# All c, x, query and gate columns of a decoder layer as pairs by seven products, with the attention beside the gates' pairs

## The chip, the cores and the metric

The kernel runs on one core of one Trainium2 chip. The metric is the device time of one execution in microseconds (us): the time before is the median of 3 runs, 964.23 us (963.68 to 964.24). The trace is of one more execution, which took 963.59 us.

The engines are named as the profile names them: PE is TensorE's matmuls and PEld its weight loads, DVE is VectorE, ACT is ScalarE, POOL is GpSimd, and SP is SyncE, which here only issues DMAs. Each engine takes its instructions in one order and waits at the first that isn't ready.

## The reference

One layer of a decoder, for a prompt of 512 tokens and 8 sequences of 8 new tokens, which are computed together as 576 columns. What matters of it here:

```
h = _rmsnorm(x, norm1_g) * (1.0 + sc1) + sh1
proj = h @ w_in
b_gate, c_gate, xa, q, k, v, ga, gb = jnp.split(proj, cuts, axis=-1)
u = c_gate * xa
uc, new_conv = _causal_conv(u, conv_buf, conv_w)
ya = (b_gate * uc) @ w_conv_out
o, k_state, v_state = attend(q, k, v, attn_sinks)
yb = o @ w_attn_out
mixed = jax.nn.sigmoid(ga) * ya + jax.nn.sigmoid(gb) * yb
x = x + g1 * (mixed @ w_mix_out)
h2 = _rmsnorm(x, norm2_g) * (1.0 + sc2) + sh2
a, val = jnp.split(h2 @ w_up, 2, axis=-1)
x = x + g2 * ((gelu(conv(a)) * val) @ w_down)
```

The model's width is 1024, so `b_gate`, `c_gate`, `xa`, `q`, `ga` and `gb` are 1024 columns each, in 8 blocks of 128; `k` and `v` are 256 columns each. Attention has 16 heads of 64 with a window of 128. The outputs are both `y`, the last two inputs of both convolutions, and the last 128 rows of keys and values. All of it is float32.

## The kernel before, in words

**Products.** Tensors lie with their 1024 columns on the partitions (8 blocks of 128, "k") and the 576 tokens along the row. Every large product is made of three passes over numbers split in a high and a low part (fp32r): high weight by high input, high by low, low by high. A weight block (raw, 128x1024, 512 KB from DRAM on SP's queue, a ring of 4) becomes `whi` by an ACT copy and `wlo` by a DVE subtraction. Where a name is in `moved`, `wlo` is instead an ACT copy of the negated `whi`, to which a DMA from POOL's queue adds the raw block in place. `whi` and `wlo` are rings of 5.

**A plain product** (`product`) gives 128 output columns: 8 k by 3 passes by 2 groups of tokens (256 and 320) = 48 matmuls.

**A pair by seven products** (`pair_product`) gives two blocks of 128 output columns (a and b), by Winograd's form of the 2x2 block product: the tokens in two halves of 288, k in two halves of 4, and seven parts of 4 k by 3 passes = 12 matmuls of 288 tokens, 84 in all, where two plain products take 96. It needs sums of the inputs, made once for the layer (`x00`, `n1`, `t2`, `x10`, `n3`, `x11`, `n4`), and sums of the two weight blocks, made for each pair on DVE (six instructions of 128x512). The weights are split as A (parts a0 and a1), B (s1 and b1), C (s2 and s4) and D (s3, half as wide). The parts run in this order, on three banks X, Y and Z, and behind each part one instruction empties or starts a bank (bank, weights, inputs, what follows):

```
(X, "a0", "x00", lambda: minus(Y, X)),
(Z, "s1", "n1", lambda: act.activation(p5, Z, AF.Copy, scale=scale)),
(Y, "s2", "t2", lambda: minus(Z, Y)),
(X, "a1", "x10", lambda: out_a0(X)),
(Y, "s3", "n3", lambda: out_b1(Y, p5, ALU.subtract)),
(Z, "s4", "x11", lambda: out_a1(Z, p5, ALU.add)),
(Y, "b1", "n4", lambda: out_b0(Y)),
```

`minus` is an ACT copy of 128x288 from one bank to the next with the sign turned; part 3 adds onto Y = -X, so it waits for the first of them, which has part 2 (s1) to run beside; part 6 adds onto Z = -Y in the same way, with parts 4 and 5 between. Both are called the minus copies below. While a pair runs, `Job.prepare` gives the splits of the next pair to its steps: A and the first sums ahead of part 1, B behind part 1, D and the second sums behind part 3, C behind parts 4 and 5. X and Y lie in the pool `mm` and in `aux`; with `apart` both are in `mm`. The transposes and scores of the attention use `aux`.

**Order of the work.** After the norm come v, k, and two plain products of queries (128 columns each, q0 and q1). Then a loop over six m (`PLAIN` = 0, 1, 2, 4, 5, 6) makes c and x of block m as two plain products, multiplies them, and starts that block's convolution. In its turns 1 to 3 stand three pairs of queries. The attention is a generator (`fill`) from which `tick` takes pieces between matmuls at a rate (.32 in the plain products, .2 in the query pairs). Then come 14 pairs (`jobs`): the b columns with the convolution's output (`branch`), the sigmoid gates (`gate_job`), and c and x of blocks 3 and 7 as two pairs (`inner_job`); then four pairs of `w_conv_out`, eight plain products of `w_attn_out`, the mix, and the feed-forward part with its own 22 convolutions. PE is held to the program's order throughout (the wrapper `InOrder`, whose line 113 stands for all engines' instructions that go through it); ACT and DVE are pinned so from the last turn of the `PLAIN` loop on, and before that a scheduler orders them.

**Gates.** A gate pair empties its banks through ACT's sigmoid into `sg` and stores it to DRAM (`sg_dram`, 288 KB from POOL's queue). `gate` loads it back as `gt`: in `conv_outs` for the convolution branch (`late` multiplies, one job later), and two products ahead in the loop over `w_attn_out`.

Of the kernel before, what the change touches and what calls it, by code (L numbers as in the profile page):

```python
# [10 lines left out]
F32 = mybir.dt.float32  # L11
# [20 lines left out]
PLAIN = (0, 1, 2, 4, 5, 6)  # L32
Q_TICKS = 8
OPS_AT = 1, 2, 3, 4
CACHE_AT = 17,18
EPS = 1e-6
NEG = -1e33
A_BUFS = 57
# [35 lines left out]
def step_kernel(ctx: ExitStack, tc: tile.TileContext, ins: dict, outs: list):  # L74
# [19 lines left out]
    def slot(s, dt=F32, shape=None):  # L94
        return ap_.tile(shape or [P, NT], dt, tag="a", name=nm(s))

# [201 lines left out]
    class EarlyOperands(PairOperands):  # L298


        def high(self):
# [5 lines left out]
            if self.kp % 2 == 0:  # L307
                for n in ("n4", "n3"):
                    made[n] = slot(n + "h", F32R), slot(n + "l", F32R)
# [4 lines left out]
            self.n3h, self.n3l = (x[:, at] for x in made["n3"])  # L314
            act.activation(self.nh, self.r[0][:, a], AF.Copy)
            act.activation(self.n3h, self.r[0][:, b], AF.Copy)
# [10 lines left out]

        def low(self):
            for lo, src, hi in (
                (self.tl, self.t, self.th), (self.nl, self.r[0][:, :HT], self.nh),  # L330
                (self.n3l, self.r[0][:, HT:], self.n3h),
            ):
                dve.tensor_tensor(out=lo, in0=src, in1=hi.bitcast(F32), op=ALU.subtract)
# [555 lines left out]
    made = {}  # L889
    for i in range(5):  # L890
        if i in OPS_AT:
            EarlyOperands(h, OPS_AT.index(i), made, xn).all_early()
# [63 lines left out]
    ps = product(weights(kpm(w_in, Q0 + P), NK), h)  # L956
    q1 = slot("q")
    nc.scalar.activation(q1, ps, AF.Copy, scale=HD**-0.5)
    queries(1, q1)
# [88 lines left out]
    def decode_scores(q, s, cV):  # L1048
        kTc = []
        for raw, v in (caches[q][:2], caches[q][2:]):  # L1050
# [9 lines left out]
            yield False  # L1060
        s += [slot("s", shape=[P, 2, 256]) for _ in range(2)]
# [125 lines left out]
    def attention():  # L1187
        units = [(hd, i) for hd in range(4) for i in range(4)]
        s, pts = {}, {}
        for n in range(len(units) + 3):  # L1190
            if n in CACHE_AT:
                cache_load(CACHE_AT.index(n))
# [11 lines left out]
        filler[1] = .35  # L1204
# [11 lines left out]
    def padded():  # L1216
        t = slot("pad", shape=[P, 594])
# [6 lines left out]
    def conv(u, w0, w1, w2, st):  # L1224

        nc.gpsimd.tensor_copy(out=b10(u)[:, :, 0:2], in_=st)
        y = slot("y", shape=[P, 594])
# [87 lines left out]
    def beside_conv():  # L1315
        yield from attention()
        filler[1] = 40 / 84
# [3 lines left out]
    fill(beside_conv(), .3)  # L1321
# [4 lines left out]
    class Job:  # L1326


        def __init__(self, mat, c, ops, outs, apart=P):
            self.mat, self.c, self.ops, self.outs, self.apart = mat, c, ops, outs, apart  # L1330
            self.before, self.after = {}, {}
# [18 lines left out]
    def branch_outs(*ms):  # L1350
        ts, ys = [slot("g") for _ in range(2)], [ycv.pop(m) for m in ms]

        def first_half(e, ps):
            dve.tensor_tensor(out=ts[e][:, :HT], in0=ps, in1=ys[e][:, :HT], op=ALU.mult)

        def second_half(e, x, y, op):
            t, v = ts[e], ys[e]
# [9 lines left out]

    def gate_outs(x, m):
        ta, tb = (slot("sg") for _ in range(2))

        def sigmoid(out, src):
            act.activation(out, src, AF.Sigmoid)

        def b1(x, y, op):
            dve.tensor_tensor(out=tb[:, HT:], in0=x, in1=y, op=op)

        def a1(x, y, op):
            sigmoid(tb[:, HT:], tb[:, HT:])
            dve.tensor_tensor(out=ta[:, HT:], in0=x, in1=y, op=op)

        def b0(ps):
            sigmoid(tb[:, :HT], ps)
            sigmoid(ta[:, HT:], ta[:, HT:])
            for e, t in enumerate((ta, tb)):
                pool.dma_start(sg_dram[x, m + e], t)

        return lambda ps: sigmoid(ta[:, :HT], ps), a1, b0, b1
# [15 lines left out]

    def gate(x, m):
# [6 lines left out]
    def conv_outs(m):  # L1411
# [4 lines left out]
            lambda t=t, g=g: dve.tensor_tensor(out=t, in0=t, in1=g, op=ALU.mult) for t, g in zip(ts, gs)  # L1416
# [37 lines left out]
    def gate_job(n):  # L1454
        x, c, m = (1, 5632, 2 * n) if n < 4 else (0, 4608, 2 * n - 8)
        return Job(w_in, c + m * P, made, lambda: gate_outs(x, m))

    jobs = [
        branch(0, 1), branch(2, 4), branch(5, 6), gate_job(0), gate_job(1), gate_job(2), inner_job(3),
        inner_job(7), gate_job(3), branch(3, 7), gate_job(4), gate_job(5), gate_job(6), gate_job(7),  # L1460
    ]
    n_conv = len(jobs)
    jobs += [Job(wco, m * P, made_g, lambda m=m: conv_outs(m)) for m in range(0, NK, 2)]


    for at, m in enumerate(PLAIN):
        if at in (4, 5):
            src, dst = ((ins["cache_k_win"], nks), (ins["cache_v_win"], nvs))[at - 4]
            tc.keep_in_program_order(
                nc.gpsimd.dma_start(  # L1470
                    dst[:, 0:120, :].rearrange("b (x w) c -> b x (w c)", x=2),
                    src[0].rearrange("b w h d -> b w (h d)")[:, 8:128, :].rearrange(
                        "b (x w) c -> b x (w c)", x=2
                    ),
                )
            )
        w = weights(kpm(w_in, 1024 + m * P), NK)
        if 1 <= at <= 3:
            qt = [slot("q") for _ in range(2)]
            filler[1] = .2  # L1480
            pair_product(q_job.w, made["op"], {}, *copy_outs(qt, HD**-0.5), True, HD**-0.5)
            filler[1] = .32
            for n in range(2):
                queries(2 * at + n, qt[n])
        if at == 5 and filler:
            filler[1] = .4
# [792 lines left out]
```

## Time and profile before

| | |
|---|---|
| time before, median of 3 runs | 964.23 us (963.68 to 964.24) |
| the profiled execution | 963.59 us |
| its span, first to last instruction | 961.5 us |
| PE / PEld busy in the span | 945.7 / 904.6 us |
| DVE / ACT / POOL busy | 713.8 / 538.4 / 120.3 us |
| granted TensorE clock | 0.997 |

The program's stretches in that execution: from 72.8 us on the plain products of c and x, with the query pairs and the attention between; from some 228 us the 14 pairs; from some 410 us the `w_conv_out` pairs, `w_attn_out` and the mix; from some 545 us the feed-forward part.

How to read the rows: names are those of the kernel without their numbers, out<-in; all seven-product and attention work goes through line 113 except what has a line of its own. A matmul's duration (295 ns for 288 tokens) is its way through the array and overlaps the next; what one costs is the distance from start to start. "Idle before" is the time an engine stood still ahead of an instruction, with the engine that ended it behind the arrow.

### The profile page before, as it was taken

The page shows a single profiled execution, that of the slowest core. Times are in us where ns is not written, and L with a number is a line of the kernel's source. Part 1 is how long each engine was busy: PE and PEld are TensorE (multiplying, and loading weights), DVE is VectorE, ACT ScalarE, POOL GpSimd, SP SyncE. Part 2 cuts the span into 40 slices and gives each one's busy share as a digit, 9 for nine tenths or more (in the row PEclk, how much of TensorE's full clock was granted, in tenths as well). Part 3 has the DMA queues.
Part 4 walks back from the last instruction along what each step waited for, and adds up shares of the span by engine and source line. Part 5 has one row for each costly group of instructions (what it writes and reads, how often), then busy time and mean ns, then how long its engine had stood idle before and what let it go on. Part 6 is the DMA issues. An engine that isn't in the chain of part 4 may idle for free.

```text
span 961.5 us, 18628 instructions
## 1 busy us (share of the span) xinstructions
PE 945.7 (98%) x7290; PEld 904.6 (94%) x7290; DVE 713.8 (74%) x1335; ACT 538.4 (56%) x1039; POOL 120.3 (13%) x297
## 2 busy tenths in 40 slices
PE   6999999999999999999999999999999999999997
PEld 5799898989899989999889999999999999999997
DVE  4786878764866767776677688995559998968874
ACT  5464647645666446875335567563226565546664
POOL 2121000101211011210001131100000001101110
PEclk9999999999999999999999999999999999999999
DMA  9992212425555768899985732332323333328542
GB/s 279 326 263 74 64 51 67 152 84 134 133 136 164 250 217 216 201 241 275 312 292 118 179 93 66 89 108 69 106 86 95 89 88 102 92 75 176 130 96 99
DMA packets 181689, 141.45 MB, mean 147 GB/s; under 512 B 7368, under 2 KB 161804, under 8 KB 181314
## 3 DMA queue, kind: packets, MB, share of 16 engines
q1 hardware_dynamic: 172546, 111.72, 38.9%
q0 software_dynamic: 8912, 28.29, 12.8%
q8 instruction: 57, 0.93, 0.4%
q14 instruction: 30, 0.25, 0.1%
q10 hardware_dynamic: 144, 0.26, 0.1%
HBM read 113.89 MB, written 12.07 MB: 131 GB/s over the span
## 4 chain that ended last, share of the span: by engine, by line
PE 71%; ACT 2%; DMA 1%; DVE 1%; issue 0%; DVEq 0%; ACTq 0%
PE mm L113 40%; PE aux L113 29%; PE aux L1270 2%; DMA wl<-s 1%; ACT whi L113 0%; ACT wlo L113 0%; ACT xh L113 0%; ACT s L1017 0%; ACT sg L113 0%; ACT nh L113 0%; DVE g L113 0%; DVE wlo L113 0%; ACT aux L113 0%; ACT p L113 0%; DVE s L1081 0%
## 5 line engine op out<-in xcount | busy, mean ns | idle before, releaser
L113 ACT ACTIVATE whi<-raw 128x1024 fp32r<-128x1024 f32 (+3 forms) x186 | 188.5, 1022 | 82.1 <-DVE raw L113 29.0
L113 DVE TENSOR_TENSOR wlo<-raw,whi 128x1024 fp32r<-128x1024 f32 (+2 forms) x163 | 192.4, 1186 | 40.9 <-ACT whi L113 40.3
L113 PE MATMUL aux<-2h,whi 128*128 128x288 f32 (+2 forms) x232 | 68.5, 295 | 0.0
L113 PE MATMUL aux<-2h,wlo 128*128 128x288 f32 (+2 forms) x232 | 68.4, 295 | 0.0
L113 PE MATMUL aux<-2l,whi 128*128 128x288 f32 (+2 forms) x232 | 68.3, 295 | 0.0
L113 DVE TENSOR_TENSOR raw<-raw 128x512 f32<-128x512 f32 x88 | 61.6, 700 | 2.8
L113 PE MATMUL mm<-hh,whi 128*128 128x256 f32 (+2 forms) x264 | 62.1, 309 | 0.5 <-ACT hh L113 0.5
L113 PE MATMUL mm<-hh,wlo 128*128 128x256 f32 (+2 forms) x264 | 58.2, 295 | 0.0
L113 PE MATMUL aux<-hh,whi 128*128 128x288 f32 (+1 forms) x196 | 57.7, 301 | 0.0
L113 PE MATMUL mm<-hl,whi 128*128 128x256 f32 (+2 forms) x264 | 57.4, 296 | 0.1
L113 PE MATMUL aux<-hl,whi 128*128 128x288 f32 (+1 forms) x196 | 56.5, 295 | 0.0
L113 PE MATMUL aux<-hh,wlo 128*128 128x288 f32 (+1 forms) x196 | 56.5, 295 | 0.0
L113 PEld LDWEIGHTS mm<-hh,whi 128*128 128x128 f32 x264 | 43.6, 188 | 6.6 <-issue 5.4
L113 PE MATMUL mm<-fh,whi 128*128 128x256 f32 x224 | 47.9, 295 | 0.1
L113 PE MATMUL mm<-fl,whi 128*128 128x256 f32 x224 | 47.9, 295 | 0.0
L113 PE MATMUL mm<-fh,wlo 128*128 128x256 f32 x224 | 47.7, 294 | 0.0
L113 PEld LDWEIGHTS mm<-hl,whi 128*128 128x128 f32 x264 | 44.0, 188 | 0.7 <-DVE hl L113 0.5
L113 PEld LDWEIGHTS mm<-hh,wlo 128*128 128x128 f32 x264 | 44.6, 188 | 0.0
L113 PEld LDWEIGHTS aux<-2l,whi 128*128 128x128 f32 x232 | 43.7, 188 | 0.0
L113 PEld LDWEIGHTS aux<-2h,whi 128*128 128x128 f32 x232 | 43.6, 188 | 0.0
L113 PEld LDWEIGHTS aux<-2h,wlo 128*128 128x128 f32 x232 | 43.6, 188 | 0.0
L113 DVE SCALAR_TENSOR_TENSOR y<-pad,par2T,y 128x592 f32<-128x592 f32 x44 | 36.7, 833 | 8.7 <-ACT y L113 7.9
(402 smaller groups left out, 3063.8 us busy)
## 6 DMA issues: line engine op xcount, KB each, us to landing
raw<-in_w_in SPq DMA_DIRECT2D x52, 512.0 KB, 4.6
raw<-in_w_up SPq DMA_DIRECT2D x44, 512.0 KB, 4.0
ada<-in_w_ada SPq DMA_DIRECT2D x64, 256.0 KB, 5.7
wlo<-raw POOLq DMA_DIRECT2D x17, 512.0 KB, 4.8
ad<-in_w_ada SPq DMA_DIRECT2D x32, 256.0 KB, 6.6
raw<-in_w_down SPq DMA_DIRECT2D x16, 512.0 KB, 4.0
sg_dram<-sg POOLq DMA_DIRECT2D x16, 288.0 KB, 4.4
gt<-sg_dram SPq DMA_DIRECT2D x16, 288.0 KB, 6.0
```

Source lines behind the costliest of these rows:

```text
L113: done = getattr(self.engine, name)(*args, **kwargs)
L1270: done = nc.tensor.matmul(ps[32 * j : 32 * j + 32, :], cT[:, k, :], cols[k][j], start=(k == 1), stop=(k == NK - 2),)
```

## The change

- c and x of all eight blocks are made by pairs (`inner_job` for m = 0 to 7: c and x of one block are the pair's two outputs). The six turns with plain products are gone, and `PLAIN` with them.
- One list of 23 pairs follows q1: gates 0, query pair 1, gates 1 and 2, query pair 2, gates 3 and 4, query pair 3, then `inner_job` and `branch` pairs, and gates 5 to 7 at the end. The four `w_conv_out` pairs follow as before.
- The attention is taken from beside these pairs (rates .28, .45 for the new tokens' part, .6 for the modulation behind it). For the first 14 (`N_ATT`) X and Y are both in `mm`, the low part of B is `moved`, and ACT and DVE are ordered by the scheduler; from the 15th on both are pinned, and the low parts of B and D are `moved`.
- Gate pairs copy raw sums to `sg` and DRAM. The sigmoid is one ACT instruction of 128x576 on each `gt` that comes back, in `late` and in the loop over `w_attn_out`.
- The split input n3 (behind x00's operands) no longer has tiles of its own: its high and low part overwrite the second halves of h's, after q1's product.
- Pads and convolution outputs (594 wide) have a pool of 5 tiles of their own; the pool of 576-wide slots goes from 57 to 54. The loads of the caches, the copies of the caches to the outputs and `state_out` move to other places.

```diff
-PLAIN = (0, 1, 2, 4, 5, 6)
+N_ATT = 14
-A_BUFS = 57
+A_BUFS = 54
+U_BUFS = 5
+    def wide(s):
+        return ap_.tile([P, 594], F32, tag="uy", name=nm(s), bufs=U_BUFS)
...
-                ("x00", h0, l0, a), ("n3", *made["n3"], at), ("x10", h1, l1, a), ("x11", h1, l1, b),
+                ("x00", h0, l0, a), ("n3", h0, l0, b), ("x10", h1, l1, a), ("x11", h1, l1, b),
...
-    fill(beside_conv(), .3)
+    fill(beside_conv(), .28)
...
+    def gate_outs(x, m):
+        ts = [slot("sg") for _ in range(2)]
+        a0, a1, b0, b1 = copy_outs(ts)
+
+        def last(ps):
+            b0(ps)
+            for e, t in enumerate(ts):
+                pool.dma_start(sg_dram[x, m + e], t)
+
+        return a0, a1, last, b1
...
         late.extend(
-            lambda t=t, g=g: dve.tensor_tensor(out=t, in0=t, in1=g, op=ALU.mult) for t, g in zip(ts, gs)
+            lambda t=t, g=g: (
+                act.activation(g, g, AF.Sigmoid), dve.tensor_tensor(out=t, in0=t, in1=g, op=ALU.mult)
+            )
+            for t, g in zip(ts, gs)
         )
...
     jobs = [
-        branch(0, 1), branch(2, 4), branch(5, 6), gate_job(0), gate_job(1), gate_job(2), inner_job(3),
-        inner_job(7), gate_job(3), branch(3, 7), gate_job(4), gate_job(5), gate_job(6), gate_job(7),
+        gate_job(0), query_job(1), gate_job(1), gate_job(2), query_job(2), gate_job(3), gate_job(4),
+        query_job(3), inner_job(0), inner_job(4), branch(0, 4), inner_job(1), inner_job(5), branch(1, 5),
+        inner_job(2), inner_job(6), branch(2, 6), inner_job(3), inner_job(7), branch(3, 7),
+        gate_job(5), gate_job(6), gate_job(7),
     ]
...
-    for at, m in enumerate(PLAIN):
...
-        ps = product(w, h)
...
-        ps = product(w, h, steps)
...
+    jobs[0].load()
+    ps = product(w_q1, h, spread_out(jobs[0].prepare()))
+    jobs[1].load()
+    q1 = slot("q")
+    nc.scalar.activation(q1, ps, AF.Copy, scale=HD**-0.5)
+    queries(1, q1)
+    for op in early_ops:
+        op.n3()
+    stT = state_in(st_conv, "stT", NK)
+    a = aux()
+    transpose(a[:, :74], par2, ident[:74, :74])
+    nc.scalar.copy(par2T, a[:, :74])
...
     for n, job in enumerate(jobs):
+        if n == N_ATT:
+            pinned += [act, dve]
...
-        steps = jobs[n + 1].prepare("BD" if n < 3 or n > 9 else "", n == n_conv) if n + 1 < len(jobs) else {}
+        steps = jobs[n + 1].prepare("B" if n < N_ATT else "BD", n == n_conv) if n + 1 < len(jobs) else {}
         outs = job.outs()
-        pair_product(job.w, job.ops["op"], joined(job.before, steps, job.after), *outs)
+        pair_product(job.w, job.ops["op"], joined(job.before, steps, job.after), *outs, n < N_ATT, job.scale)
...
         t = gb.pop(m)
+        act.activation(t, t, AF.Sigmoid)
```

**ACT after q1's product.** In the rows below `q` is the copy of q1's result, `mm<-mm` is Y = -X of a pair with both banks in `mm`, `p<-aux` the copy of Z to p5, `aux<-mm` Z = -Y, and the rows of line 1017 or 1009 are the exponentials of the attention. Before, ACT went from q1's copy to the first plain product's c, and on to the first query pair:

```order
L958 ACTIVATE q_952<-mm_903 128x576
L1495 COPY c_1034<-mm_981 128x576
L995 COPY stT<-aux_1031 128x128
L113 ACTIVATE whi_1066<-raw_1044 128x1024
L113 ACTIVATE whi_1112<-s_1047 128x512
L113 ACTIVATE whi_1130<-raw_1042 128x1024
L113 ACTIVATE whi_1159<-raw_1157 128x1024
L113 ACTIVATE y_1153<-pad_1146,parT 128x592
L1017 ACTIVATE s_1075,den_1091<-s_1075,nmx_1087 128x128 x2
L1017 ACTIVATE s_1076,den_1091<-s_1076,nmx_1087 128x128 x2
L1023 ACTIVATE es_1092<-es_1092 128x4
L113 ACTIVATE mm_1166<-mm_1165 128x288
L113 ACTIVATE p_1168<-aux_1167 128x288
```

With the change, ACT goes from q1's copy to the first gate pair. `whi_972` is that pair's C; `whi_1026` and `whi_1043` are A and B of the second pair, `wlo_1044` the negated copy for B's low part; `wh` and `whi_1093` are D and C of the second pair; `sg` are the copies of the first pair's results:

```order
L1493 ACTIVATE q_992<-mm_918 128x576
L987 COPY stT<-aux_1007 128x128
L117 ACTIVATE whi_972<-raw_914 128x1024
L117 ACTIVATE whi_1026<-raw_988 128x1024
L117 ACTIVATE whi_1043<-raw_990 128x1024
L117 ACTIVATE wlo_1044<-whi_1043 128x1024
L1500 COPY par2T<-aux_1010 128x74
L117 ACTIVATE mm_1020<-mm_1019 128x288
L117 ACTIVATE p_1022<-aux_1021 128x288
L117 ACTIVATE wh_1074<-s_1023 128x512
L117 ACTIVATE aux_1021<-mm_1020 128x288
L117 ACTIVATE whi_1093<-raw_988 128x1024
L117 ACTIVATE sg_1017<-mm_1019 128x288
```

Behind q1's copy stand six instructions ahead of the first Y = -X, four of them 1024 wide; before there was a whole c and x product between.

**ACT in the third and fourth pair (gates 1 and 2), beside the attention.** The rows run from the copies of the second pair's results (`q`) to the minus copies of the third (`mm_1332<-mm_1331`, `aux_1333<-mm_1332`); `whi_1338`, `whi_1355` and `wlo_1356` are A and B of the fourth pair, `s`, `es` and `pt` attention:

```order
L117 ACTIVATE q_908<-mm_1142 128x288
L117 ACTIVATE whi_1338<-raw_1138 128x1024
L117 ACTIVATE whi_1355<-raw_1140 128x1024
L117 ACTIVATE q_909<-mm_1143 128x288
L117 ACTIVATE wlo_1356<-whi_1355 128x1024
L117 ACTIVATE mm_1332<-mm_1331 128x288
L1009 ACTIVATE s_1266,den_1282<-s_1266,nmx_1278 128x256 x2
L1009 ACTIVATE s_1267,den_1282<-s_1267,nmx_1278 128x256 x2
L1015 ACTIVATE es_1283<-es_1283 128x4
L117 ACTIVATE p_1334<-aux_1333 128x288
L117 ACTIVATE wh_1416<-s_1335 128x512
L117 ACTIVATE aux_1333<-mm_1332 128x288
L1156 COPY pt_1430<-aux_1425 128x512
```

The splits of the pair after are now in the same queue as the exponentials and the minus copies; before, no splits of a further pair were prepared inside a query pair, only those of the next plain product.

**ACT where the convolution's gates return.** The rows stand in the second `w_conv_out` pair: `mm<-aux` is its Y = -X, `gt` the two gates that `late` multiplies, `whi_5359` and `wlo_5360` B of the third pair:

```order
L117 ACTIVATE whi_5340<-raw_5191 128x1024
L117 ACTIVATE mm_5334<-aux_5333 128x288
L117 ACT_TABLE_LOAD
L117 ACTIVATE gt_5195<-gt_5195 128x576
L117 ACTIVATE whi_5359<-raw_5193 128x1024
L117 ACTIVATE wlo_5360<-whi_5359 128x1024
L117 ACTIVATE p_5336<-aux_5335 128x288
L117 ACTIVATE gt_5197<-gt_5197 128x576
L117 ACTIVATE aux_5335<-mm_5334 128x288
L117 ACTIVATE wh_5392<-s_5337 128x512
```

Before, the load of the sigmoid's table and the sigmoids stood in the first gate pair:

```order
L113 ACTIVATE mm_3434<-aux_3433 128x288
L113 ACTIVATE whi_3459<-raw_3264 128x1024
L113 ACTIVATE p_3436<-aux_3435 128x288
L1098 COPY pt_3491<-aux_3486 128x512
L113 ACTIVATE aux_3435<-mm_3434 128x288
L113 ACTIVATE wh_3503<-s_3437 128x512
L113 ACT_TABLE_LOAD
L113 ACTIVATE sg_3431<-aux_3433 128x288
L1098 COPY pt_3533<-aux_3528 128x512
L113 ACTIVATE whi_3522<-raw_3262 128x1024
L113 ACTIVATE sg_3432<-sg_3432 128x288
L113 ACTIVATE sg_3432<-mm_3434 128x288
L113 ACTIVATE sg_3431<-sg_3431 128x288
L113 ACTIVATE whi_3589<-raw_3427 128x1024
```

The table load and two sigmoids of 576 are now ahead of p5 and of Z = -Y in the second `w_conv_out` pair. The number of table loads is 4 in both.

More of the change, by code (lines that the diff above doesn't have):

```diff
@@ L955, in step_kernel @@
     queries(0, q0)
[L956 to L959, printed above, removed]
+    w_q1 = weights(kpm(w_in, Q0 + P), NK)
     nd = V[2][:, 1, :]
@@ L1216, in padded @@
     def padded():
-        t = slot("pad", shape=[P, 594])
+        t = wide("pad")
         nc.gpsimd.memset(t[:, 0:2], 0.0)
@@ L1366, in branch_outs @@
         )
[L1368 to L1387, printed above, removed]
     def copy_outs(ts, scale=1.0):
@@ L1456, in gate_job, with query_job, outs, last @@
         return Job(w_in, c + m * P, made, lambda: gate_outs(x, m))
+    def query_job(at):
+        qt = [slot("q") for _ in range(2)]
+        def outs():
+            a0, a1, b0, b1 = copy_outs(qt, HD**-0.5)
+            def last(ps):
+                b0(ps)
+                for n in range(2):
+                    queries(2 * at + n, qt[n])
+            return a0, a1, last, b1
+        return Job(w_in, Q0 + 2 * at * P, made, outs, scale=HD**-0.5)
     jobs = [
-        branch(0, 1), branch(2, 4), branch(5, 6), gate_job(0), gate_job(1), gate_job(2), inner_job(3),
@@ L1548, in step_kernel @@
     for n, at in plan.items():
-        jobs[n + 2].after = {p: g_list(names) for p, names in at.items()}
+        jobs[n + 11].after = {p: g_list(names) for p, names in at.items()}
     for n in range(4):
```

116 lines of the change are left out of this document (38 added, 78 removed).

## The prediction

> **What bounds the kernel now.** I read four views: the page's busy times with its chain of waits, PE's waits, the busy times by stretch, and then single rows. First the page: engines over the span, and the chain by engine.
>
> ```profile
> PE 945.7 (98%) x7290; PEld 904.6 (94%) x7290; DVE 713.8 (74%) x1335; ACT 538.4 (56%) x1039; POOL 120.3 (13%) x297
> ...
> PE 71%; ACT 2%; DMA 1%; DVE 1%; issue 0%; DVEq 0%; ACTq 0%
> ```
>
> PE is busy for 945.7 of 961.5 us, and the chain is made of its matmuls. Time goes only where matmuls go, or where PE is made to wait. Its waits (line waited for, total us, times, longest):
>
> ```profile
> PE aux L113 <- POOL ident masks.py:199: 4.4, 1, 4.4
> PE aux L113 <- POOL rs L113: 1.8, 1, 1.8
> PE mm L113 <- ACT mm L113: 0.7, 1, 0.7
> PE mm L113 <- DVE g L113: 0.7, 1, 0.7
> ...
> PE aux L1174 <- ACT pt L1162: 0.5, 1, 0.5
> ```
>
> 6.2 us of waiting are at the start, which the change doesn't touch. "ACT mm" is a minus copy that came late. The stretches show where DVE and ACT are near their limit (us; PE, PEld, DVE, ACT, POOL busy; clock; DMA):
>
> ```profile
> 80.00:200.00 120.00, 120.00 (x923) 108.45 (x922) 95.28 (x263) 73.63 (x215) 8.35 (x25) 1.00 0.27 80
> 200.00:228.00 28.00, 27.51 (x211) 24.84 (x211) 15.02 (x36) 14.70 (x44) 1.79 (x6) 1.00 0.40 113
> 228.00:320.00 92.00, 90.53 (x780) 86.80 (x779) 65.11 (x110) 55.80 (x113) 15.92 (x33) 1.00 0.60 162
> 600.00:640.00 40.00, 40.00 (x304) 40.00 (x303) 38.32 (x61) 24.39 (x41) 3.50 (x13) 1.00 0.32 93
> ```
>
> From 80 to 200 us, plain products and query pairs beside the attention, PE stands still for nothing although DVE is at 79% and ACT at 61%. From 600 to 640 us it doesn't either, with DVE at 96%. From 200 to 320 us, where the attention's end and the first of the 14 pairs are, it loses 28.00 - 27.51 + 92.00 - 90.53 = 2.0 us.
>
> **Matmuls removed.** Twelve plain products become six pairs. The pace of both, from PE's instructions in the first plain product of c (start, duration), and from pieces of the chain in the feed-forward part (start, length, count):
>
> ```profile
> 72.78 0.43 PE L113 MATMUL mm<-hh,whi 128*128 128x256 f32 x2
> ...
> 78.85 0.43 PE L113 MATMUL mm<-hh,wlo 128*128 128x256 f32 x2
> ```
>
> ```profile
> 613.58 3.17 PE aux L113 x24
> ...
> 624.69 3.17 PE aux L113 x24
> ...
> 656.47 52.35 PE mm L113 x396
> ```
>
> The first two rows are the first and the last of 24 couples (256 and 320 tokens): 6.07 us for 23 steps, 0.264 us each, 6.33 us a product. The next two are the same part of two neighbouring pairs, 11.11 us apart. Twelve products are 76.0 us, six pairs 66.7 us: **-9.3 us**. By the third row, 72 matmuls of 132.2 ns, it would be 9.5 us. The other matmuls stay: the same attention, gates, queries and branches in another order.
>
> **Work added on DVE and ACT.** A pair needs six sums of 128x512 on DVE, which a plain product doesn't, and splits D besides A, B and C; the B splits of the jobs beside the attention go from DVE to ACT.
>
> ```profile
> L113 ACT ACTIVATE whi<-raw 128x1024 fp32r<-128x1024 f32 x170 | 178.2, 1054 | 76.3 <-DVE raw L113 29.0 <-PE mm L113 21.5 <-DMA raw<-in_w_down 10.7
> L1017 ACT ACTIVATE s<-s,nmx 128x256 f32<-128x256 f32 x56 | 27.8, 501 | 10.3 <-DVE nmx L1011 10.3
> L113 ACT ACTIVATE wlo<-whi 128x1024 fp32r<-128x1024 f32 x17 | 18.0, 1060 | 0.4
> L113 ACT ACTIVATE aux<-mm 128x288 f32<-128x288 f32 x44 | 17.4, 395 | 40.6 <-PE mm L113 39.9 <-ACT whi L113 0.5
> L113 ACT ACTIVATE fh<-cy 128x576 fp32r<-128x576 f32 x22 | 14.8, 679 | 16.4 <-DVE cy L113 15.5 <-POOL pad L1842 0.9
> L113 ACT ACT_TABLE_LOAD x4 | 5.1, 1283 | 0.8 <-PEq L2264 0.7
> L113 DVE TENSOR_TENSOR wlo<-raw,whi 128x1024 fp32r<-128x1024 f32 x153 | 186.4, 1222 | 39.6 <-ACT whi L113 39.0
> L113 DVE TENSOR_TENSOR raw<-raw 128x512 f32<-128x512 f32 x88 | 61.6, 700 | 2.8
> wlo<-raw POOLq DMA_DIRECT2D x17, 512.0 KB, 4.8
> ```
>
> By these, with the counts of both programs: sixteen more negated copies 17 us of ACT, six more highs 6 us, nine more half-wide ones 6 us, sigmoids of 576 instead of 288 some 4 us; about 33 us more on ACT in all. DVE gets 24 sums more (17 us), ten full low parts fewer (12 us) and eight half-wide ones more (6 us), some 10 us in all. Neither engine is full: the whole span would have ACT at 59% and DVE at 75%. Beside the attention a pair's 11.1 us of PE with some 4.6 us of attention has 13 to 15 us of DVE work, much as in the stretch from 80 to 200 us; that is why I cost the bulk of it at **nothing**. The cover is thin, though: if it fails, each pair is late by what DVE lacks, at most 0.5 us by these figures.
>
> **The first pair after q1** is where I find a wait. Its Y = -X follows part 1 and is needed when part 2 ends. In ACT's queue stand q1's copy, a small copy, four 1024-wide instructions (C of this pair, A, B and negated B of the next) and another small copy. The same kinds of rows in the trace (start, duration):
>
> ```profile
> 72.98 0.65 ACT L958 ACTIVATE q<-mm 128x576 f32<-128x576 f32 x1 [1.59 <-PE mm L113]
> 79.31 0.64 ACT L1495 COPY c<-mm 128x576 f32<-128x576 f32 x1 [5.68 <-PE mm L113]
> 79.85 0.27 ACT L995 COPY stT<-aux 128x128 f32<-128x128 f32 x1
> 80.01 1.07 ACT L113 ACTIVATE whi<-raw 128x1024 fp32r<-128x1024 f32 x1
> 80.97 0.63 ACT L113 ACTIVATE whi<-s 128x512 fp32r<-128x512 f32 x1
> ```
>
> From a 576-wide copy to the next start 0.54 us, past the small one 0.16, past a full split 0.96. So 72.98 + 0.54 + 0.16 + 4 x 0.96 + 0.13 = 77.65 for the start of Y = -X, and 78.05 for its end (0.40). PE starts part 1 at about 72.85; a part is 12 x 0.132 = 1.59 us, so part 3 could start at 76.05. **+2.0 us**. Below, if the scheduler's order lets ACT begin the splits under q1's product: nothing; above, if B's sum (0.70) on DVE comes late as well: 2.7. I take 2.0, since the order has q1's copy ahead of all four. Behind it stand p5 and the splits of the next pair, which then have 11 us.
>
> **The pairs behind it.** ACT's order has one 288-wide copy and the negated B ahead of each next Y = -X: 0.4 + 1.0 us, done before part 1 ends at 1.6; the copy itself then has 1.6 - 0.4 = 1.2 us of slack. How a query pair fared beside the attention before, in ACT's rows:
>
> ```profile
> 89.79 0.19 ACT L1023 ACTIVATE es<-es 128x4 f32<-128x4 f32 x1
> 89.88 0.39 ACT L113 ACTIVATE mm<-mm 128x288 f32<-128x288 f32 x1
> 91.06 0.41 ACT L113 ACTIVATE p<-aux 128x288 f32<-128x288 f32 x1 [0.79 <-PE aux L113]
> ```
>
> The minus copy came right behind exponentials with no idle time in front of it, so it was in the queue's way, and PE lost nothing. For small waits I use the rate of the stretch in which pairs stood beside the attention before: 2.0 us in 120 us. The attention with its pairs now lasts from 73 to about 285 us, 212 us: 3.5 us, of which 2.0 are in the old time already: **+1.5 us**. The bounds are -2.0 (all of it goes) and +7, half a microsecond in each of 14 pairs.
>
> **The gates' return.** The load of the sigmoid's table and two sigmoids now stand in the second `w_conv_out` pair, ahead of Z = -Y: behind Y = -X at 1.6 us come 0.4, 1.28, 0.6, two B instructions 1.9, p5 0.3, the sigmoid 0.6 and Z = -Y 0.4, so about 7.2 us into a pair that wants it at part 6, 8.0 us. **Nothing**, with 0.8 us to spare; the eight sigmoids beside `w_attn_out` have whole products of 6.3 us. [...]
>
> **The sum**, on the profiled execution: 963.59 - 9.3 + 2.0 + 1.5 = 957.8 us. That execution is 0.6 us under the median of 964.23 and inside 0.1%, so I don't correct for it. I forecast **957.5 us**.
>
> **Rivals.**
>
> *All of the saving, no new waits* (953 us). For it: no idle time from 80 to 200 us with both engines as loaded, and the 96% of DVE from 600 us on. Against it: ACT's order after q1. 963.6 - 9.3 = 954.3, and 952.3 if the old 2.0 us go too.
>
> *The late stages lose some* (960.5 us). Sigmoids, table load and the pool of five 594-wide tiles, which pads and convolution outputs of the feed-forward part now share, turn into waits. The profile shows the feed-forward pairs at 11.11 us without a gap; each of its 22 convolutions holds a pad and an output. At 0.13 us for each of 22 it is 3 us more: 957.5 + 3.
>
> *The minus copies come late in every pair beside the attention* (968 us, the other side). Its place is Y = -X in the 13 pairs after the first. The copy's slack of 1.2 us goes where a high copy of B, which waits for a sum on DVE, stops ACT's queue: 29.0 us of idle time stand in the row of `whi<-raw` above against DVE's sums, so such waits do happen. If DVE is one split and one sum behind (1.22 + 0.70), the copy is 0.7 us late; if four exponentials (4 x 0.49) come in besides, 1.2 us or more. 13 x 0.7 to 13 x 1.2 is 9 to 16 us on 963.6 - 9.3 + 2.0 = 956.3: 965 to 972. From 0.56 us a pair on it eats the saving. Against it: the query pairs beside the attention before, and the splits' buffers, which let a pair's splits be ready a pair ahead.
>
> *The change in count does not reach the end*: the attention, now in a denser mix, does not end within its pairs and is left over. ACT's order has its last exponentials ahead of the 17th of 23 pairs, so it would need six pairs of delay. 963 to 967 us.
>
> **How the numbers follow.** Forecast (955 to 960) 0.48; no new waits 0.17; late stages 0.13; minus copies late 0.17; attention left over 0.05. A measurement of this kernel tells about 0.2% (1.9 us) from no change: faster is under 962.3, slower over 966.2. Faster: the first two and two thirds of the third, 0.48 + 0.17 + 0.09 = 0.74. Same: 0.04 of the third, 0.04 of the fourth, 0.02 of the last, 0.10. Slower: 0.13 + 0.03 = 0.16. The range is 952 to 966, which leaves out the upper part of the fourth and a little of the fifth.
>
> **What would show it.** PE's matmuls fall by 72; DVE's busy time rises by about 10 us and ACT's by about 33. In PE's waits "mm <- ACT mm" grows by about 2 us in one piece between 70 and 80 us; PE's idle time from 80 to 290 us is near 3.5 us, none over 0.7 us. From 300 us on each pair is 11.1 us. The forecast is wrong if "mm <- ACT mm" has ten or more entries (the minus copies), if waits for DVE's `wlo` or `raw` sum to over 4 us, if waits for the DMA `wlo<-raw` appear, or if the feed-forward part, 540 us to the end before, gets longer.

## The result, and the profile after

The changed kernel takes **980.2 us** (978.47 to 983.16, 4 runs) against 963.95 us before: 1.0174 times as long, 95% interval 1.0148 to 1.0200. The forecast was 957.5 us, in a range of 952 to 966. It is wrong by 23 us and in its sign.

The profiled execution took 978.47 us, its span 976.7 us: 15.2 us more than before. The page of the changed kernel, busy times and chain by engine:

```profile
PE 944.2 (97%) x7218; PEld 900.6 (92%) x7218; DVE 723.6 (74%) x1366; ACT 571.7 (59%) x1086; POOL 143.3 (15%) x320
...
PE 88%; DMA 5%; ACT 4%; DVE 1%; issue 1%; SPq 0%; ACTq 0%; DVEq 0%; POOLq 0%
```

The 72 matmuls are gone (7290 to 7218), DVE has 10 us more and ACT 33 us more, all as forecast. But PE's busy time fell by 1.5 us only. The shares of the chain can't be set against those of before: the chain shown there covers 75% of the span and this one nearly all of it, and E8 below, which is faster than both, has 5% of DMA in its chain as well. By stretch (the columns of the prediction; 330 to 430 us of the kernel before, then the changed kernel):

```profile
330.00:430.00 100.00, 99.82 (x755) 94.55 (x754) 75.49 (x116) 65.69 (x113) 19.13 (x29) 1.00 0.81 222
```

```profile
0.00:72.00 72.00, 63.38 (x515) 54.08 (x516) 49.12 (x100) 39.05 (x86) 18.56 (x49) 0.98 0.93 276
72.00:90.00 18.00, 16.15 (x111) 15.92 (x110) 13.32 (x24) 10.37 (x17) 3.20 (x6) 0.91 0.63 168
90.00:330.00 240.00, 237.80 (x1901) 219.93 (x1901) 188.16 (x441) 164.88 (x404) 45.46 (x77) 1.00 0.55 141
...
330.00:360.00 30.00, 27.29 (x208) 24.02 (x207) 18.41 (x28) 15.99 (x24) 7.73 (x17) 1.00 0.94 255
360.00:400.00 40.00, 32.36 (x222) 27.37 (x220) 17.09 (x29) 14.07 (x24) 5.91 (x9) 0.96 0.72 202
400.00:430.00 30.00, 27.41 (x192) 27.16 (x193) 24.41 (x41) 24.52 (x43) 7.56 (x10) 0.94 0.78 207
```

From 330 to 430 us PE stands still for 2.71 + 7.64 + 2.59 = 12.9 us, where it stood still for 0.2 before. Neither DVE nor ACT is loaded there: they wait too. The sum of the 15.2 us: matmuls removed -9.5; this idle time +12.7; the first pair's wait +1.85; the granted clock +5.1 (an estimate from the trace's clock records: three stretches of 3.41 us at half clock, from 78.8, 392.9 and 403.1 us, which the kernel before doesn't have, and each of which takes 1.7 us; they are the 0.91, 0.96 and 0.94 of the rows); the start +1.1 (up to q1 all changed kernels here are the same, and PE's busy time there is 63.2 to 65.1 us); 430 to 560 us +0.9; some 3 are left over, for which see the matmuls under "The other terms".

PE's waits in the changed kernel:

```profile
PE mm L117 <- ACT aux L117: 6.9, 5, 4.4
PE mm L117 <- ACT mm L117: 6.0, 3, 3.4
...
PE aux L1264 <- DMA ada<-in_w_ada: 4.3, 2, 2.7
```

Line 1264 is the modulation: its matmuls wait for blocks of `w_ada`. The first two rows are minus copies that came late; of their 12.9 us, 7.8 lie between 330 and 430 us and 1.85 in the first pair, and only 2.2 beside the attention. What they are behind is in the waits of ACT, DVE and SP's queue, the first two in 330 to 430 us, SP's in 335 to 420 us:

```profile
ACT th L117 <- DMA sg_dram<-sg: 7.1, 1, 7.1
```

```profile
DVE tl L117 <- PE aux L1264: 13.1, 1, 13.1
```

```profile
SPq L156 <- DMA wlo<-raw: 54.6, 6, 13.5
SPq L1280 <- DMA sg_dram<-sg: 7.0, 1, 7.0
```

`th` and `tl` are operands of the `w_conv_out` pairs. ACT may not write `th` before a gate's store to DRAM has been read out of the same tile; DVE may not write `tl` before PE has used up a block of `w_ada` in it. SP's queue (line 156 weights, 1280 blocks of `w_ada`) stands behind an accumulating DMA that still reads a raw block, and then behind the same store. ACT and DVE are held to the program's order there, so the minus copies and splits behind `th` and `tl` stop as well: from 330 to 430 us PE waits 4.4 us for one Z = -Y and 3.4 us for one Y = -X. SP's rows alone prove nothing, since the kernel before has nearly the same in that window, with 0.2 us of idle time on PE:

```profile
SPq L152 <- DMA wlo<-raw: 42.7, 5, 11.4
SPq L1286 <- DMA sg_dram<-sg: 6.9, 1, 6.9
```

What is new are the waits for `ada` on PE, and those of `th` and `tl`: before, `th` waited 2.6 us and `tl` 2.3, for other things. From the chain (start, length; short pieces left out):

```profile
353.00 4.26 DMA ada<-in_w_ada
...
367.63 4.75 DMA ada<-in_w_ada
...
378.42 3.81 DMA wl<-s
...
382.70 1.22 DVE wlo L117
383.92 0.38 DVE sg L117
...
384.85 4.09 DMA sg_dram<-sg
...
389.63 0.39 ACT sg L117
390.02 0.94 ACT whi L117
390.97 0.31 ACT mm L117
391.32 2.04 PE mm L117 x12
```

First two loads of `w_ada` that PE itself waits for. Then an accumulating DMA, a gate's result, its store, and ACT goes on to the minus copy that PE waits for.

### The profile page after: what moved, and what is told of

Its sections match the earlier page's. It is cut to its first block, busy times and chain, and to the rows that moved or that the text cites. A ratio compares the mean times of both kernels' runs of the same rounds, so it can differ in the third digit from the quotient of the medians.

```text
span 976.7 us, 18605 instructions
## 1 busy us (share of the span) xinstructions
PE 944.2 (97%) x7218; PEld 900.6 (92%) x7218; DVE 723.6 (74%) x1366; ACT 571.7 (59%) x1086; POOL 143.3 (15%) x320
## 4 chain that ended last, share of the span: by engine, by line
PE 88%; DMA 5%; ACT 4%; DVE 1%; issue 1%; SPq 0%; ACTq 0%; DVEq 0%; POOLq 0%
PE mm L117 50%; PE aux L117 35%; DMA ad<-in_w_ada 2%; PE aux L1264 1%; PE aux L1168 1%; ACT whi L117 1%; DMA ada<-in_w_ada 1%; ACT s L1009 1%; DMA raw<-in_w_in 1%; DMA x<-in_x_prompt 1%; ACT wlo L117 0%; DMA sg_dram<-sg 0%; DMA wl<-s 0%; DVE wlo L117 0%; ACT aux L117 0%
## 5 line engine op out<-in xcount | busy, mean ns | idle before, releaser
L117 ACT ACTIVATE whi<-raw 128x1024 fp32r<-128x1024 f32 (+3 forms) x192 | 194.8, 1023 | 113.4 <-DVE raw L117 35.3
L117 DVE TENSOR_TENSOR wlo<-raw,whi 128x1024 fp32r<-128x1024 f32 (+3 forms) x153 | 180.2, 1184 | 32.1 <-ACT whi L117 31.7
L117 DVE TENSOR_TENSOR raw<-raw 128x512 f32<-128x512 f32 x100 | 70.1, 701 | 2.5
L117 PE MATMUL aux<-2h,whi 128*128 128x288 f32 (+2 forms) x232 | 68.6, 296 | 0.0
L117 PE MATMUL aux<-2h,wlo 128*128 128x288 f32 (+2 forms) x232 | 68.5, 295 | 0.0
L117 PE MATMUL aux<-2l,whi 128*128 128x288 f32 (+2 forms) x232 | 68.5, 295 | 0.0
L117 POOL DMA_DIRECT2D wlo<-raw x39 | 34.4, 881 | 183.5 <-ACT wlo L117 64.7
L117 PE MATMUL aux<-hh,whi 128*128 128x288 f32 (+2 forms) x180 | 54.2, 308 | 0.0
L117 PE MATMUL aux<-hh,wlo 128*128 128x288 f32 (+2 forms) x180 | 52.7, 300 | 0.0
L117 PE MATMUL aux<-hl,whi 128*128 128x288 f32 (+2 forms) x180 | 52.7, 300 | 0.0
L117 PE MATMUL mm<-fh,wlo 128*128 128x256 f32 x224 | 47.7, 294 | 0.0
L117 PE MATMUL mm<-fh,whi 128*128 128x256 f32 x224 | 47.7, 294 | 0.0
L117 PE MATMUL mm<-fl,whi 128*128 128x256 f32 x224 | 47.1, 292 | 0.0
L117 PE MATMUL mm<-hh,whi 128*128 128x288 f32 (+2 forms) x160 | 45.4, 307 | 0.5 <-ACT hh L117 0.5
L117 PE MATMUL mm<-t,whi 128*128 128x288 f32 x184 | 40.0, 308 | 6.0 <-ACT mm L117 6.0
L117 PEld LDWEIGHTS aux<-2h,whi 128*128 128x128 f32 x232 | 43.6, 188 | 0.0
L117 PEld LDWEIGHTS aux<-2l,whi 128*128 128x128 f32 x232 | 43.6, 188 | 0.0
L117 PEld LDWEIGHTS aux<-2h,wlo 128*128 128x128 f32 x232 | 43.5, 188 | 0.0
L117 DVE SCALAR_TENSOR_TENSOR y<-pad,par2T,y 128x592 f32<-128x592 f32 x44 | 36.6, 833 | 9.0 <-ACT y L117 8.2
L117 PE MATMUL mm<-hh,wlo 128*128 128x288 f32 (+2 forms) x160 | 43.3, 295 | 0.0
L117 PE MATMUL mm<-hl,whi 128*128 128x288 f32 (+2 forms) x160 | 42.7, 298 | 0.0
L117 ACT ACTIVATE aux<-mm 128x288 f32<-128x288 f32 x50 | 19.9, 397 | 36.8 <-PE mm L117 36.0
```

Source lines behind the costliest of these rows:

```text
L117: done = getattr(self.engine, name)(*args, **kwargs)
```

## The experiments

Two theories for 330 to 430 us. **T1, tiles**: the modulation, the gates and the operands of `w_conv_out` share 54 tiles and wait for each other, because the attention ends later and with it the modulation. **T2, the raw ring**: accumulating DMAs hold the raw blocks longer, SP's queue stands, and what is behind in it comes late. Gains are counted from the changed kernel's 980.2 us, whose own runs lie up to 4.7 us apart; the kernel before, measured again with each group of experiments, stayed between 963.95 and 964.72 us.

**E1, one block of w_ada.**

```diff
-                cols[k][j] = slot("ada", shape=[P, 512])
-                c = c0 + 512 * j
-                nc.sync.dma_start(cols[k][j], ins["w_ada"][0, k * P : k * P + P, c : c + 512])
+                if n == 0 or c0 != 2048:
+                    cols[k][j] = slot("ada", shape=[P, 512])
+                    c = c0 + 512 * j
+                    nc.sync.dma_start(cols[k][j], ins["w_ada"][0, k * P : k * P + P, c : c + 512])
+                else:
+                    cols[k][j] = cols[0][0]
```

> The modulation beside the pairs loads one block of w_ada and uses it 32 times (31 loads of 256 KB and their tiles are left out, so its modulation values are not the reference's; its 64 matmuls stay). Theory T1 (tiles): from 330 to 430 us the loads of the modulation, the operands of w_conv_out and the gates' raw sums want the same 54 tiles, and ACT and DVE, in program order there, stop at the first that is not free. T1 expects PE's idle time from 330 to 430 us to fall from 12.9 us to under 3 us and the median to 963 to 968 us. Theory T2 (the raw ring): SP's queue stands behind weight loads that wait for the accumulating DMAs (54.6 us of such waits from 335 to 420 us), so weights come late. T2 expects weights to be late still: idle time over 6 us, 972 us or more.

Measured: 963.53 us (961.71 to 964.43, 10 runs), 16.7 us less than the changed kernel. The same stretches:

```profile
330.00:360.00 30.00, 30.00 (x219) 23.34 (x218) 13.92 (x23) 12.90 (x21) 6.74 (x14) 1.00 0.54 123
360.00:400.00 40.00, 39.45 (x296) 38.18 (x296) 31.70 (x53) 28.11 (x46) 10.46 (x15) 1.00 0.70 170
400.00:430.00 30.00, 28.57 (x212) 28.08 (x211) 23.29 (x37) 23.52 (x40) 5.58 (x8) 1.00 0.92 229
```

2.0 us of idle time are left of 12.9, and the clock is full. SP's weight loads still wait 79.6 us for accumulating DMAs from 320 to 430 us, more than the 65.2 of the changed kernel, and PE hardly waits. So the modulation's loads and tiles are needed for the loss; weights that come late are not its cause by themselves. E1 also takes away the traffic of 31 loads; E8 below keeps that traffic and is faster still, so it isn't the traffic.

**E2, B's low part on DVE from the 15th pair on.**

```diff
-        steps = jobs[n + 1].prepare("B" if n < N_ATT else "BD", n == n_conv) if n + 1 < len(jobs) else {}
+        steps = jobs[n + 1].prepare("B" if n < N_ATT else "D" if n < n_conv else "BD", n == n_conv) if n + 1 < len(jobs) else {}
```

> From the 15th pair to the last before w_conv_out the low part of B is made by DVE's subtraction again (as it is D that stays an accumulating DMA), so that no raw block waits for an accumulating DMA there. T2 expects the idle time of 330 to 430 us to fall under 4 us and the median to 965 to 970 us. T1 expects 977 us or more: the same tiles, with 1.2 us more of DVE in each of 8 pairs.

Measured: 972.68 us (972.18 to 975.8), 7.5 us less. Neither theory's number. SP's wait for accumulating DMAs (320 to 430 us) shrinks from 65.2 us, though it now waits 32.5 us for DVE's work on the raw blocks; PE's wait for the modulation's loads is gone, but ACT's wait for the gates' store stays:

```profile
SPq L156 <- DMA wlo<-raw: 9.3, 1, 9.3
```

```profile
ACT th L117 <- DMA sg_dram<-sg: 9.0, 1, 9.0
```

From 360 to 400 us PE still loses 7.8 us. T2 holds for a part.

**E3, the work beside the pairs earlier, by higher rates.**

```diff
-    fill(beside_conv(), .28)
+    fill(beside_conv(), .34)
-        filler[1] = .45
+        filler[1] = .8
-        filler[1] = .6
+        filler[1] = .9
```

> The rates at which pieces are taken from beside the pairs go up: attention .28 to .34, the new tokens' part .45 to .8, the modulation .6 to .9. In ACT's order the modulation's last copy then stands ahead of the first operand of w_conv_out. Nothing is left out. T1 expects the idle time of 330 to 430 us to fall under 4 us and the median to 964 to 970 us, with up to 3 us of new small waits before 330 us. T2 expects no gain, 977 us or more, since the weight loads still wait for the accumulating DMAs.

Measured: 969.77 us (967.99 to 972.67), 10.4 us less. T1's number, but not its stretch: PE's idle time is 5.4 us from 330 to 430 us and another 4.2 us from 270 to 330 us, where the modulation now runs; PE waits 5.1 us for its loads. That fits loads which at .9 are asked for faster than SP's queue delivers them; it was not tested.

**E4, the first minus copy ahead of the splits.** In the first pair ACT is pinned and the next pair's A and B are emitted a part later.

```diff
+        if n == 0:
+            pinned += [act]
+        if n == 1:
+            pinned.remove(act)
...
-        steps = jobs[n + 1].prepare("B" if n < N_ATT else "BD", n == n_conv) if n + 1 < len(jobs) else {}
+        steps = jobs[n + 1].prepare("B" if n < N_ATT else "BD", n in (0, n_conv)) if n + 1 < len(jobs) else {}
```

> In the first pair ACT is held to the program's order and the splits A and B of the second pair are emitted one part later, so that the first Y = -X stands ahead of three 1024-wide ACT instructions. The wait there cost 1.85 us of idle time, and the granted clock from 72 to 90 us was 0.91, which is 1.6 us more if the clock drop follows from the wait. Both theories on 330 to 430 us expect nothing there. If the wait also causes the clock drop: 976 to 977 us, clock 1.00 from 72 to 90 us. If the clock drop has another cause: 978 to 979 us. If the splits come late in its place: no change.

Measured: 976.39 us (975.73 to 976.52), 3.8 us less, all four runs under the lowest of the changed kernel. The stretch from 72 to 90 us:

```profile
72.00:90.00 18.00, 18.00 (x138) 17.57 (x137) 15.79 (x32) 12.38 (x21) 4.62 (x8) 1.00 0.56 148
```

PE stands still for nothing there, and the clock is full. The wait of 1.85 us is gone, and with it up to 1.7 us of clock.

**E5, one tile more.**

```diff
-A_BUFS = 54
-U_BUFS = 5
+A_BUFS = 55
+U_BUFS = 4
```

> One tile more in the pool that the loads of the modulation, the operands of w_conv_out, the gates and the attention share (54 to 55), one 594-wide tile fewer (5 to 4). Nothing is left out. T1 (tiles): the wait of th for the gates' store (7.1 us) and of tl for the modulation's matmuls (13.1 us) get shorter, 974 to 978 us against 980.2; with no loss in the feed-forward part if four 594-wide tiles do. T2 (the raw ring): 980 us. If four are too few, the stretch from 560 us on gets longer by more than 2 us.

Measured: 970.94 us (968.95 to 973.73), 9.3 us less, more than T1 expected. The feed-forward part, counted from its first product, is not longer for the 594-wide tile it lost (401.3 us, 400.9 in the changed kernel). SP's wait for accumulating DMAs nearly stays (59.6 us from 320 to 430 us, 65.2 in the changed kernel), while ACT's wait at `th` falls from 7.1 to 3.7 us and DVE's at `tl` from 13.1 to 6.7. So one tile more than 54 is worth 9 us here, and it is T1's resource. PE still waits 4.4 us for the modulation's loads.

**E6, the query pairs first.** All rates as in the changed kernel; the order of the first eight pairs:

```diff
-        gate_job(0), query_job(1), gate_job(1), gate_job(2), query_job(2), gate_job(3), gate_job(4),
-        query_job(3), inner_job(0),
+        query_job(1), gate_job(0), query_job(2), gate_job(1), query_job(3), gate_job(2), gate_job(3),
+        gate_job(4), inner_job(0),
```

> The query pairs are the 1st, 3rd and 5th of the list, not the 2nd, 5th and 8th, with all rates as they were, so that the attention waits less for its queries. In ACT's order the modulation's last copy then stands beside the first operand of w_conv_out, as in the kernel before, and not 26 rows behind it. T1 expects PE's idle time from 330 to 430 us to fall from 12.9 to under 6 us and the median to 969 to 974 us. T2 expects the same late weight loads, 978 us or more.

Measured: 969.74 us (968.28 to 971.83), 10.5 us less; the idle time from 330 to 430 us is 6.7 us, somewhat over the 6 that T1 allowed. Why: the attention takes its pieces at a fixed rate and lets a turn pass when the next head's queries are not there. With the query pairs 2nd, 5th and 8th it lost turns: at the same rates the modulation's first load is issued at 323 us in the changed kernel and at 304 us here. So the modulation was pushed into the operands of `w_conv_out`.

**E7, the floor: E1 and E4 together.**

> E1 and E4 together: one block of w_ada used 32 times, and the first minus copy ahead of the splits (the modulation's values are again not the reference's). If the two losses are separate, 963.5 - 3.8 = 959.7 us. If the first pair's wait hides a later one, 961.5 us or more. What is then still over 954.7 us (964.0 - 9.3) is neither of the two.

Measured: 960.81 us (959.86 to 962.17). The two losses add up to within 1.1 us. 5.9 us remain over the 954.9 that the matmuls alone would give.

**E8, a whole kernel**: E2, E4, E6, and the rates .32, .6, .6.

> A whole kernel, nothing left out: the query pairs early (E6), the first minus copy ahead (E4), the low part of B on DVE from the 15th pair on (E2), and rates .32 / .6 / .6, with which the modulation's last copy stands 21 rows ahead of the first operand of w_conv_out in ACT's order. By T1 and T2 together both losses go and it comes near the floor: 960 to 964 us. If the denser attention costs DVE or ACT what the tiles give, 966 us or more.

Measured: **960.67 us** (960.49 to 961.29), 0.9958 of the kernel before (95% interval 0.9941 to 0.9975): it beats both kernels, and comes to the same time as E7 with nothing left out.

```profile
72.00:90.00 18.00, 18.00 (x139) 17.59 (x137) 16.11 (x36) 12.77 (x21) 4.82 (x8) 1.00 0.64 158
90.00:330.00 240.00, 236.75 (x1888) 214.08 (x1887) 185.26 (x425) 159.22 (x395) 40.01 (x74) 1.00 0.59 164
330.00:430.00 100.00, 98.03 (x733) 95.67 (x732) 82.50 (x125) 64.15 (x107) 16.43 (x28) 1.00 0.61 161
```

The modulation's loads are now issued from 277 to 326 us, where they cost 1.3 us of PE's waits. DVE is at 83% from 330 to 430 us, and PE loses 2.0 us there, as in E1.

**E9, the returned gates later.** From the first to the last copy of `ya` the four `w_conv_out` pairs take 39.0 us in the changed kernel and 37.6 before, 1.4 us more. The chain in its second pair (the piece "ACT L117" is the table load):

```profile
434.37 1.28 ACT L117
435.66 0.69 ACT gt L117
436.35 0.96 ACT whi L117
...
438.30 0.39 ACT p L117
...
439.16 0.41 ACT aux L117
439.57 0.04 issue
439.61 1.87 PE mm L117 x12
```

The pair begins at about 432.3 us, and Z = -Y ends 7.2 us into it, just where the prediction had it. Yet PE waited, 0.9 us; the last line is its part 5.

```diff
-                1: [lambda n=n: late[2 * n - 2]()], 2: [lambda n=n: late[2 * n - 1]()],
+                3: [lambda n=n: late[2 * n - 2]()], 4: [lambda n=n: late[2 * n - 1]()],
```

> E8, and the two returned gates of each w_conv_out pair go through the sigmoid behind parts 3 and 4, not behind 1 and 2, so that they and the table load stand behind Z = -Y in ACT's order. In the changed kernel and in E8 the four w_conv_out pairs take 39.0 us from the first to the last copy of ya against 37.6 us before; theory T3: part 5 adds onto the bank Y, which Z = -Y still has to read, so Z = -Y is wanted at the end of part 4, 6.4 us into the pair, and not at part 6; it ends at 7.2 us. T3 expects 37.6 to 38.0 us there and 0.9 to 1.4 us less in all, 959.5 us. If the sigmoids stay in the way of something else: no change, 960.7.

Measured: 961.49 us (960.14 to 964.0, 11 runs), not less than E8, and the four pairs take 39.6 us: T3 expected 959.5 and at most 38.0. The wait for Z = -Y falls from 1.3 to 0.4 us in PE's waits, and a new one takes its place:

```profile
PE mm L117 <- DVE ya L117: 1.4, 2, 1.0
```

T3 was right on what PE waited for, but the edit only moved the wait. Before, PE waited 0.2 us in these pairs, so the wait explains 0.7 of the 1.4 us; the rest stays open.

**E10 and E11, tiles with and without E2's part.** E10 is E9 with 55 and 4 tiles; E11 is E10 with B's low part as an accumulating DMA from the 15th pair on, as in the changed kernel.

> E9 with 55 tiles of 576 and 4 of 594. If tiles still bound it in 330 to 430 us (2.0 us of idle time in E8): 957.5 to 959 us. If the collision is gone with the earlier modulation: within 0.5 us of E9.

> E10 without E2's part: the low part of B is an accumulating DMA again from the 15th pair on. If the raw ring matters once the tiles suffice (T2), the modulation's loads come late again and PE waits for them: 2 us or more above E10. If it was only the tiles: within 1 us of E10, or faster, since DVE has 1.2 us less in each of 8 pairs.

Measured: 960.97 us (959.8 to 961.68) and 969.92 us (966.63 to 971.67). With the modulation early the tile is worth 0.5 us, no more than these runs can tell. But the accumulating DMAs cost 9 us: SP waits 84.7 us for them from 320 to 430 us, and PE waits for the modulation's loads again, 3.6 us of it ahead of 330 us:

```profile
PE aux L1264 <- DMA ada<-in_w_ada: 5.3, 4, 2.3
```

So T2 is no rival of T1 but its other half: the modulation's loads need a tile (E5) and a turn in SP's queue (E2, E11), and the changed kernel was short of both.

**E12, the loss made in the kernel before.** Only the modulation is slower there:

```diff
-        filler[1] = 40 / 84
+        filler[1] = .4
```

> The kernel before, with the modulation beside its pairs taken at a rate of .40, not .476, and nothing else. In ACT's order the modulation's last copy then stands behind the second operand copy (th) of w_conv_out, not ahead of it. T1 (the collision of tiles, which needs no pairs for c and x) expects PE's idle time from 330 to 430 us to go from 0.2 us to 3 us or more, and 967 to 972 us against 964. If the collision needs the changed kernel's 54 tiles: 964 us.

Measured: 973.82 us (973.1 to 975.29), 1.0095 of the kernel before (1.0081 to 1.0109): 9.3 us from one number, more than the 967 to 972 us that T1 expected, in a program with plain products for c and x and 57 tiles.

```profile
330.00:430.00 100.00, 92.86 (x682) 85.78 (x681) 68.36 (x107) 60.47 (x104) 17.42 (x27) 0.95 0.75 206
```

```profile
PE aux L1270 <- DMA ada<-in_w_ada: 7.1, 1, 7.1
```

7.1 us of idle time in place of 0.2, at a clock of 0.95. The kernel before stood close to this edge all the time; the change pushed the modulation over it.

## Why the prediction was wrong, step by step

**The step that failed** is the sentence "The other matmuls stay: the same attention, gates, queries and branches in another order", which put the whole move of the work beside the pairs at nothing. The attention with its pairs was said to last "from 73 to about 285 us"; it lasted to 323 us (its last exponentials to 297), and the modulation behind it, which the prediction never placed, issued its loads from 323 to 393 us. Before, they were issued from 301 to 368 us, ahead of the first operands of `w_conv_out` (first `th` at 371.6 us; in the changed kernel at 364.1). What a later attention makes late next was not followed: the modulation's 32 loads, SP's queue and the cut from 57 tiles to 54 were not in the sum. What the runs showed in place of that nothing: 12.9 us of idle time from 330 to 430 us, and a collision that costs 16.7 us (E1).

**The rival that came nearest** was "the change in count does not reach the end", by an attention that ends late. It named the late end, dismissed it since the last exponentials stand ahead of the 17th of 23 pairs, and priced only an attention left over at the end. It is not the attention that was late for its user, but what stands behind it in the same generator.

**The other terms.**

- Matmuls, -9.3 us. The count was right. In E7 and E8, where the clock is as before, PE's busy time is 5.9 and 5.2 us lower, not 9.5. Worked out from the start times of PE's instructions between 73 and 405 us, a pair's matmul follows the last after 137 ns in E7 and E8, not 132: behind each piece of attention or modulation, and behind each wait, a step takes about 0.23 us and not 0.13, some 70 times. The pairs before had less of it (134.9 ns), and the plain products, at 138, were not at 132 either. The pace of 11.11 us, taken from the undisturbed feed-forward part, was too good for pairs that are broken into. This was read from traces and not tested by an experiment of its own.
- The first pair, +2.0 us: right. ACT's rows:

```profile
73.51 0.65 ACT L1493 ACTIVATE q<-mm 128x576 f32<-128x576 f32 x1 [2.14 <-PE mm L117]
74.06 0.26 ACT L987 COPY stT<-aux 128x128 f32<-128x128 f32 x1
74.20 2.96 ACT L117 ACTIVATE whi<-raw 128x1024 fp32r<-128x1024 f32 x3
77.20 1.06 ACT L117 ACTIVATE wlo<-whi 128x1024 fp32r<-128x1024 f32 x1
78.16 0.20 ACT L1500 COPY par2T<-aux 128x74 f32<-128x74 f32 x1
78.26 0.40 ACT L117 ACTIVATE mm<-mm 128x288 f32<-128x288 f32 x1
```

  Y = -X starts 4.75 us behind q1's copy; 4.67 were forecast. PE lost 1.85 us. What was missing is the clock behind it (see the last section).
- The pairs beside the attention, +1.5 us: PE stands still for 2.2 us from 90 to 330 us, against 2.0 before, so it was +0.2. "The minus copies come late in every pair", to which 0.17 was given and which would have had the right sign, did not happen; of the 13 pairs three show a wait of 0.6 to 0.8 us. The time it gave, 965 to 972 us, was too low as well.
- The gates' return, nothing: it was 0.9 us of waiting, in pairs that are 1.4 us longer. Z = -Y ended at 7.2 us as worked out, but the prediction set its limit at part 6, which reads Z, 8.0 us. Part 5 adds onto Y, which Z = -Y still has to read, so the limit is the end of part 4, 6.4 us. E9 shows that the wait goes with the order of the sigmoids, and that another, for `ya`, comes in its place.
- DVE's density was no bound: 83% from 330 to 430 us in E8, where PE lost 2.0 us.
- "The late stages lose some" did not come true: the feed-forward part takes 400.9 us from its first product to the end, and took 400.6.
- The forecast of 957.5 us is 0.3 under the sum of 957.8, without a term for it; beside 23 us that changes nothing.

## What to carry to other kernels

When a stage is rebuilt, list what runs *beside* it and behind that, down to the last load, and find where each now ends against the first instruction that needs the same tiles and the same queue; here a generator's tail cost nearly twice what the rebuilt stage could gain. A pool that just suffices is a schedule: the kernel before lost 9 us by a rate of .40 in place of .476, and the changed kernel won 9 us by one more tile. And a copy between accumulation banks has two limits, the reader of its result and the next writer of its source; here the earlier one decided, the writer at 6.4 us and not the reader at 8.0: the copy ended at 7.2 us, and PE waited 0.9 us.

## What the runs showed of the hardware

The same wait of 1.85 us in the first pair was followed by a slow clock in some executions and not in others: from 72 to 90 us the changed kernel's profile, E1's and E3's show a granted clock of 0.91 and 111 to 113 matmuls, and E2's, E5's and E6's the same idle time, a clock of 1.00 and 124 matmuls. E2's row beside the changed kernel's above:

```profile
72.00:90.00 18.00, 16.15 (x124) 15.64 (x123) 14.25 (x30) 11.38 (x18) 4.63 (x8) 1.00 0.65 181
```

So this wait had a second price, some 1.7 us (13 matmuls of 0.132 us), paid in three executions of six. The clock records of the changed kernel show it as half the clock for 3.41 us, once, from 0.1 us behind the wait's end; in that stretch a matmul of 288 tokens follows the last after 0.24 us, and behind it after 0.13 us:

```profile
78.83:82.24 3.41, 3.41 (x15) 3.41 (x16) 1.39 (x3) 0.93 (x3) 0.69 (x1) 0.50 1.11 255
```

What decides whether it is paid was not shown; no run moved the wait on purpose. The four stretches at half clock in the changed kernel's trace are 3.41 us long each and start at 17.39, 78.83, 392.86 and 403.10 us: 61.44, 314.03 and 10.24 us from one to the next, which is 18, 92 and 3 times 3.413. The length of a wait alone does not decide: the one that ends at 357.3 us in the changed kernel is 2.71 us long, and the clock is 1.00 from there to 392 us.
